# Opening: products of ones ahead of the first row, a row moved; a norm's root on VectorE and two holds dropped

## The chip, the cores and the metric

The kernel runs on one core of a Trainium2 chip. The engines are TensorE (PE; its weight loads are listed as PEld), VectorE (DVE), ScalarE (ACT), GpSimd (POOL) and SyncE (SP, used here for its DMA queue). The metric is device time of one execution in microseconds; the time before is a median of three runs.

## The reference

Two layers of a diffusion transformer with model width 1024 on 256 latent tokens (LAT) and 256 context tokens (CTX), all in fp32. Cut to what matters:

```python
mod_lat = split(silu(c) @ ada_w[i] + ada_b[i], 9)        # shift, scale, gate for three sublayers
mod_ctx = split(silu(c_ctx) @ ada_w[i] + ada_b[i], 9)
def half_ffn(h, shift, scale, gate, w_in, w_out, g, b):
    xm = h * (1 + scale) + shift
    a, u = split(xm @ w_in, 2)
    y = (silu(a) * u) @ w_out
    return layer_norm(ALPHA * h + 0.5 * gate * y, g, b)
# layer 0: half_ffn, grouped-query attention (+ post norm), half_ffn
# layer 1: half_ffn, mLSTM (+ post norm), half_ffn; h_lat is returned
layer_norm(x) = (x - mean) * rsqrt(var + 1e-5) * g + b
```

The FFN's hidden width is 2816. The four FFNs are called first to fourth here; the norm behind the second one ends layer 0, and the norm behind the third one stands ahead of the mLSTM.

## The kernel before, in words

**Layout and products.** The hidden state is kept transposed in SBUF, h[128, 8, 512]: eight tiles of 128 features, with columns 0 to 255 for LAT and 256 to 511 for CTX. Every matrix product is made as three fp32r products: high half of the weights by high half of the input, high by low, and low by high (`mm3`, L230, L233, L234). A weight tile is split by `split`: ACT writes the high half as a cast (L213), DVE subtracts it from the original to get the low half (L218), in one piece or in four slices of 256 columns. Raw weight tiles stand in a ring of four (`RAW`); SP issues their DMAs in order (L198), each waiting until the last slice of an earlier split has read the tile that it overwrites. The split pairs stand in a ring of seven.

**The opening (`start`).** The rows of silu(c) for LAT (v = 0) and CTX (v = 1) are needed on all 128 partitions, for dot products on DVE. PE spreads them (`replicate(v, i)`: four fp32 products of 128 columns for each half i of row v, into the PSUM tile rep[v][i]), and DVE copies them to SBUF (`replicated`, L1525). The shift (ch 0) and scale (ch 1) vectors of the first sublayer are then made tile by tile: some by PE (`by_pe`, eight fp32 products of two columns for each vector tile), the others by DVE dots (`by_dve`, L1542). With these, ACT and DVE modulate the input tile (`modulated`, L1555; low half at L1560), and `products(d)` makes 21 products of 512 columns for tile d with the first weights. Each fp32 product stands as two rows in the trace. The program order of PE, DVE and ACT is pinned by hand in this function.

**The norm behind an FFN (`norm`).** It is a generator; the last output units of the FFN and the first input units of the next one advance it by one step at places that tables of letters give. Its steps for each half (LAT, then CTX): the mean by PE; eight tiles of subtraction (DVE, L447) and squares (ACT, L454), summed by DVE or POOL (L466); the variance by PE; the root of its inverse for 256 tokens, as a 128 x 2 tile; a product of the identity with it (L492); PE spreads it over the partitions; eight tiles of scaled and modulated input with high and low halves (L517 to L524). The residual of the FFN's last units is added at L626 and summed at L402. The root is made in one of two ways: `root_log` on ACT with Ln and Exp (L271, L272) and one Newton step of three DVE operations (L273 to L275), for which ACT has to load another table (L262) and later the one for Silu again (L570); or `rsqrt_half` on DVE, an integer guess and three Newton steps of three operations. Which one is used is set by `log`: "load" loads the table ahead, "kept" uses what is loaded, and no entry takes DVE. The norm behind the second FFN uses "load" for LAT and "kept" for CTX.

**The hold (`tie`).** With `tie`, the last square of the LAT half becomes a fence: each later split's cast on ACT is ordered behind that square (`behind`, an edge of order only). The norms behind the second and the third FFN have it. Work that is not pinned is ordered by a tile scheduler.

## Time and profile before

| what | value |
|---|---|
| timed runs | 1642.85, 1645.7, 1650.05 us; median 1645.7 |
| profiled execution: time | 1653.1 us |
| profiled execution: span of the core | 1651.0 us |
| mean granted TensorE clock | 0.994 |
| PE busy | 1622.1 us (98%) |
| DVE busy | 1407.1 us (85%) |
| ACT busy | 751.8 us (46%) |
| POOL busy | 160.0 us (10%) |

The profile is of one execution of its own, not of a timed run; its time is the span and 2.1 us around it. A product of PE is listed with its full duration, though products overlap, so a pace is read from the number of rows in a stretch rather than from the mean duration. The granted clock is a share of full speed. In a row of a wait, the arrow points to what the engine waited for; in a row of the timeline, the bracket holds the idle time ahead of the row and what ended it.

### The profile page before, as it was taken

How to read it: one execution, taken by the hardware profiler on the slowest of the kernel's cores; microseconds unless marked ns; L12 is line 12 of the kernel's file. 1: busy time of each engine (PE TensorE's matmuls, PEld its weight loads, DVE VectorE, ACT ScalarE, POOL GpSimd, SP SyncE). 2: the span in 40 equal slices, each digit the busy share in tenths (PEclk: the TensorE clock that was granted, in tenths of full speed). 3: DMA queues.
4: the chain of work that ended last, by engine and by line, in shares of the span. 5: the costliest groups of instructions: out<-in, count | busy, mean ns of one | idle time of the engine just before them, and what ended most of it. 6: DMA issues, size and time to landing. Idle time of an engine off the chain costs nothing. (4 is left out here: it accounts for less than half of the span.)

```text
span 1651.0 us, 27330 instructions
## 1 busy us (share of the span) xinstructions
PE 1622.1 (98%) x10496; PEld 1475.7 (89%) x10496; DVE 1407.1 (85%) x2857; ACT 751.8 (46%) x1369; POOL 160.0 (10%) x237
## 2 busy tenths in 40 slices
PE   9999999999999999999999899999999999999998
PEld 8888888889988998899999898998999978999986
DVE  6899999979788998888796899898797967997686
ACT  4532123315676364254354453453453646556542
POOL 0011111102321200000000200000001002120000
PEclk9999999999999999999999899999999999999999
DMA  7777777732202444435333544335332342437552
GB/s 283 269 247 252 229 243 237 247 128 87 65 1 79 177 167 149 145 103 179 115 114 105 192 153 141 115 111 183 99 119 78 109 141 77 130 114 255 180 180 75
DMA packets 72210, 250.65 MB, mean 152 GB/s; under 512 B 7952, under 2 KB 11024, under 8 KB 72080
## 3 DMA queue, kind: packets, MB, share of 16 engines
q1 hardware_dynamic: 53360, 182.93, 33.0%
q0 software_dynamic: 17856, 65.02, 12.1%
q8 instruction: 82, 1.34, 0.3%
q10 hardware_dynamic: 864, 0.96, 0.2%
q14 instruction: 48, 0.39, 0.1%
HBM read 247.83 MB, written 1.05 MB: 151 GB/s over the span
## 5 line engine op out<-in xcount | busy, mean ns | idle before, releaser
L233 PE MATMUL t<-t,t 128*128 128x256 f32 (+2 forms) x2072 | 678.5, 329 | 1.2 <-DVE t L524 0.8
L234 PE MATMUL t<-t,t 128*128 128x256 f32 (+2 forms) x2072 | 674.6, 327 | 4.7 <-DVE t L218 4.6
L230 PE MATMUL t<-t,t 128*128 128x256 f32 (+2 forms) x2072 | 676.9, 329 | 1.8 <-ACT t L213 1.7
L213 ACT CAST t<-t 128x1024 fp32r<-128x1024 f32 (+2 forms) x390 | 329.2, 866 | 309.0 <-PE t L234 134.1
L218 DVE TENSOR_TENSOR t<-t,t 128x256 fp32r<-128x256 f32 (+2 forms) x726 | 415.8, 614 | 44.8 <-ACT t L213 43.0
L234 PEld LDWEIGHTS t<-t,t 128*128 128x128 f32 x2072 | 391.4, 189 | 39.9 <-DVE t L218 5.5
L233 PEld LDWEIGHTS t<-t,t 128*128 128x128 f32 x2072 | 392.6, 190 | 37.3 <-DVE t L524 1.7
L230 PEld LDWEIGHTS t<-t,t 128*128 128x128 f32 x2072 | 390.6, 190 | 38.1 <-ACT t L213 3.2
L827 PEld LDWEIGHTS t<-t,t 128*128 128x128 f32 x2436 | 288.4, 189 | 2.6 <-ACT t L835 0.6
L827 PE MATMUL t<-t,t 128*128 128x256 f32 x2436 | 289.4, 281 | 0.6 <-DVE t L848 0.4
L338 DVE SCALAR_TENSOR_TENSOR t<-t,t 128x1024 bf16<-128x1024 f32 x224 | 266.0, 1220 | 1.3 <-DMA t<-in_ada_w 1.1
L762 ACT CAST t<-t 128x512 fp32r<-128x512 f32 (+1 forms) x116 | 108.7, 941 | 148.4 <-DVE t L764 93.6
L330 POOL DMA_DIRECT2D t<-in_ada_w x124 | 66.5, 536 | 796.0 <-DVE t L338 734.5
L763 DVE TENSOR_TENSOR t<-t,t 128x512 fp32r<-128x512 f32 (+1 forms) x116 | 125.3, 1087 | 6.8 <-ACT t L762 6.1
L626 DVE SCALAR_TENSOR_TENSOR t<-t,t,t 128x256 f32<-128x256 f32 x128 | 56.7, 478 | 52.6 <-PE t L234 52.3
L1042 PE MATMUL t<-t,t 128*128 128x256 f32 (+1 forms) x256 | 78.2, 306 | 1.1 <-DVE t L218 1.1
L1041 PE MATMUL t<-t,t 128*128 128x256 f32 (+1 forms) x256 | 78.8, 309 | 0.0
L1043 PE MATMUL t<-t,t 128*128 128x256 f32 (+1 forms) x256 | 78.3, 308 | 0.0
L570 ACT ACTIVATE t<-t 128x256 f32<-128x256 f32 (+1 forms) x64 | 30.1, 479 | 104.0 <-PE t L234 101.0
L1496 PE MATMUL t<-t,t 128*128 128x512 f32 (+2 forms) x280 | 61.3, 381 | 3.2 <-ACT t L316 3.2
L1496 PEld LDWEIGHTS t<-t,t 128*128 128x128 f32 x280 | 53.7, 236 | 10.4 <-ACT t L316 3.2
L976 PE MATMUL t<-t,t 128*128 128x512 f32 x264 | 60.0, 389 | 0.0
(198 smaller groups left out, 1481.9 us busy)
## 6 DMA issues: line engine op xcount, KB each, us to landing
t<-in_ffn_in SPq DMA_DIRECT2D x168, 512.0 KB, 4.4
t<-in_ada_w POOLq DMA_DIRECT2D x124, 512.0 KB, 4.3
t<-in_ffn_out SPq DMA_DIRECT2D x68, 512.0 KB, 4.4
t<-in_ffn_last SPq DMA_DIRECT2D x22, 512.0 KB, 3.4
t<-in_ada_w SPq DMA_DIRECT2D x15, 512.0 KB, 8.3
t<-in_att_in SPq DMA_DIRECT2D x12, 512.0 KB, 3.9
t<-in_att_out SPq DMA_DIRECT2D x8, 512.0 KB, 3.4
t<-in_ml_qk SPq DMA_DIRECT2D x8, 512.0 KB, 3.7
```

Source lines behind the costliest of these rows:

```text
L213: self.behind(self.nc.scalar.copy(h, x))
L218: self.behind(self.nc.vector.tensor_tensor(out=ls, in0=xs, in1=hs.bitcast(F32), op=ALU.subtract))
L230: ins = mm(out, wh, xh, start=first, stop=False)
L233: mm(out, wh, xl, start=False, stop=False)
L234: mm(out, wl, xh, start=False, stop=last)
L338: ins = nc.vector.scalar_tensor_tensor(self.tmp().bitcast(BF16), r, 1.0, self.cb[:, v, :], ALU.mult, ALU.mult, accum_out=to)
L762: high = lambda p, r: pin(S.copy(p[0], r))
L763: low = lambda p, r: pin(V.tensor_tensor(out=p[1], in0=r, in1=p[0].bitcast(F32), op=ALU.subtract))
L827: pin(nc.tensor.matmul(o, p, q, start=first and k == i == 0, stop=k == half - 1 and i == 2, skip_group_check=True))
L1041: mm(o, self.xh[:, k, c], wh, start=k == 0, stop=False)
L1043: mm(o, self.xl[:, k, c], wh, start=False, stop=k == ND - 1)
L1496: mm = lambda *k, **kw: pin(nc.tensor.matmul(*k, **kw))
```

## The change

There are three parts. **(A)** In the opening, eight fp32 products of the constant ones by ones, 128 x 128, are put ahead of the first `replicate`; they write rep[1][1], which the second row of c overwrites later. Both halves of c's second row are replicated behind the scale vector's products (ch 1) and ahead of the shift vector's (ch 0), where one half stood behind each; DVE's copy of the last half moves ahead of the first weights' split. **(B)** The norm behind the second FFN makes its root with `rsqrt_half` on DVE for both halves, so no table is loaded for it, and its hold is dropped. **(C)** The norm behind the third FFN keeps its root on ACT and drops its hold. The parameter `tie` goes. The line numbers behind the edits move by one or two (L1496 becomes L1494, L1525 becomes L1523, L466 becomes L464, L492 becomes L490, L517 becomes L515, L626 becomes L624).

```diff
--- before.py
+++ after.py
@@ -418,7 +418,7 @@
             else:
                 self.advance(len(self.running) - 1 if c.isupper() else 0)
 
-    def norm(self, g, coef, keep=True, nxt=True, alone=False, log=False, tie=False):
+    def norm(self, g, coef, keep=True, nxt=True, alone=False, log=False):
 
 
         nc, V, S = self.nc, self.nc.vector, self.nc.scalar
@@ -451,9 +451,7 @@
                 S.activation(xh, z, AF.Copy, scale=c)
                 V.scalar_tensor_tensor(self.xl[:, d, TL:T], z, c, xh.bitcast(F32), ALU.mult, ALU.subtract)
             q = self.tmp(w)
-            square = S.activation(q, z, AF.Square)
-            if tie and d == ND - 1:
-                self.fence = {square.ins.engine: square}
+            S.activation(q, z, AF.Square)
             if d in (SQA if alone else SQPE):
                 sums[d] = q, q
                 continue
@@ -1530,7 +1528,8 @@
             for k in range(ND):
                 mm(o[ch], raws[d][ch][:, k * P : (k + 1) * P], b.ct[:, k, :], start=k == 0, stop=k == ND - 1)
             if ch in behind:
-                replicate(*behind[ch])
+                for i in range(2):
+                    replicate(behind[ch], i)
         for ch in o:
             pin(S.activation((e0, c0)[ch][:, :, d], o[ch], AF.Identity, bias=bias(ch, d)))
 
@@ -1564,18 +1563,20 @@
             for n, o in enumerate(acc):
                 mm(o, ws[d][w][:, n * P : (n + 1) * P], b.x(d, BOTH)[x], start=not d and not i, stop=d == ND - 1 and i == 2)
 
+    for i in range(ND):
+        mm(rep[1][1][:, :P], b.ones, b.ones, start=True, stop=True)
     for i in range(2):
         replicate(0, i)
         replicated(0, i)
     load_dots(0)
     load(0)
-    by_pe(0, {1: (1, 0), 0: (1, 1)})
-    replicated(1, 0)
+    by_pe(0, {1: 1})
+    for i in range(2):
+        replicated(1, i)
     low(ws[0][2], ws[0][0], ws[0][1])
     load_dots(1)
     rows = by_dve(1)
     next(rows)
-    replicated(1, 1)
     xs = {0: modulated(0)}
     for d in range(ND):
         n = d + 1
@@ -1662,9 +1663,9 @@
         tick.done = done
         return tick
 
-    def norm(key, coef, keep=(True, True), nxt=True, alone=False, log={LAT: "load", CTX: "kept"}, tie=False):
+    def norm(key, coef, keep=(True, True), nxt=True, alone=False, log={LAT: "load", CTX: "kept"}):
         get = once(key, coef)
-        b.begin = lambda g: b.norm(g, get, keep[0 if g == LAT else 1], nxt, alone, log.get(g), tie and g == LAT)
+        b.begin = lambda g: b.norm(g, get, keep[0 if g == LAT else 1], nxt, alone, log.get(g))
 
     both = (LAT, CTX)
     feeds = [feed(q, dots, 0 if i else ROOM[0][1]) for i, (q, dots) in enumerate(zip(queue, DOTS))]
@@ -1676,10 +1677,10 @@
     b.attention(lambda: b.shift_(0, 5))
     cpool = b.silu_c()
     b.pending = [lambda: b.silu_load(lambda ins: b.after(ins, b.silu) if ins.ins.engine == b.silu.ins.engine else ins)]
-    norm("n2", lambda: b.ln_mod(0, 2, (1, 0)), tie=True)
+    norm("n2", lambda: b.ln_mod(0, 2, (1, 0)), log={})
     b.ffn(0, 1, once("g1", lambda: b.half_gate(0, 8)), both, feeds[1])
     feeds[1].done()
-    norm("n3", lambda: b.ln_mod(1, 0, (1, 3)), (True, False), log={LAT: "load"}, tie=True)
+    norm("n3", lambda: b.ln_mod(1, 0, (1, 3)), (True, False), log={LAT: "load"})
     b.ffn(1, 0, once("g2", lambda: b.half_gate(1, 2)), both, feeds[2])
     feeds[2].done()
     cpool.close()
```

PE in the opening, before: t_86 to t_89 are the four halves of c's two rows, t_97 the shift and scale vectors, t_90 the first product of the input.

```order
L1496 MATMUL t_86<-t_70,t_72 128x128 x4
L1496 MATMUL t_87<-t_70,t_72 128x128 x4
L1496 MATMUL t_97<-t_72,t_111 128x2 x8
L1496 MATMUL t_88<-t_70,t_72 128x128 x4
L1496 MATMUL t_97<-t_72,t_111 128x2 x8
L1496 MATMUL t_89<-t_70,t_72 128x128 x4
L1496 MATMUL t_97<-t_72,t_147 128x2 x8
L1496 MATMUL t_90<-t_68,t_117 128x512
```

The same place after:

```order
L1494 MATMUL t_89<-t_61 128x128 x8
L1494 MATMUL t_86<-t_70,t_72 128x128 x4
L1494 MATMUL t_87<-t_70,t_72 128x128 x4
L1494 MATMUL t_97<-t_72,t_119 128x2 x8
L1494 MATMUL t_88<-t_70,t_72 128x128 x4
L1494 MATMUL t_89<-t_70,t_72 128x128 x4
L1494 MATMUL t_97<-t_72,t_119 128x2 x8
L1494 MATMUL t_97<-t_72,t_156 128x2 x8
L1494 MATMUL t_90<-t_68,t_125 128x512
```

The ones stand first; t_88 and t_89, the second row, are now both ahead of the second run of eight two-column products, so two such runs (and the tile behind, t_156) stand in a line ahead of the products.

ACT at the LAT half of the norm behind the second FFN, before: L454 are the squares, L213 the casts of the next FFN's weights, L271 and L272 the root.

```order
L213 CAST t_9158<-t_9156 128x1024
L454 ACTIVATE t_9180<-t_67 128x256
L454 ACTIVATE t_9183<-t_67 128x256
L454 ACTIVATE t_9188<-t_67 128x256
L454 ACTIVATE t_9191<-t_67 128x256
L454 ACTIVATE t_9196<-t_67 128x256
L454 ACTIVATE t_9200<-t_67 128x256
L454 ACTIVATE t_9204<-t_67 128x256
L454 ACTIVATE t_9234<-t_67 128x256
L213 CAST t_9493<-t_9491 128x1024
L213 CAST t_9525<-t_9523 128x1024
L271 ACTIVATE t_9263<-t_9256 128x2
```

The same place after:

```order
L213 CAST t_9166<-t_9164 128x1024
L213 CAST t_9505<-t_9503 128x1024
L454 ACTIVATE t_9187<-t_67 128x256
L454 ACTIVATE t_9190<-t_67 128x256
L454 ACTIVATE t_9195<-t_67 128x256
L454 ACTIVATE t_9198<-t_67 128x256
L213 CAST t_9537<-t_9535 128x1024
L454 ACTIVATE t_9203<-t_67 128x256
L454 ACTIVATE t_9207<-t_67 128x256
L454 ACTIVATE t_9211<-t_67 128x256
L454 ACTIVATE t_9241<-t_67 128x256
L213 CAST t_9599<-t_9597 128x1024
```

The first of the next FFN's casts (t_9505) stands ahead of the squares and the second (t_9537) between the fourth and the fifth; the two rows of the root are gone, and the table load (L262), which stood three rows ahead of the first piece, too.

DVE at the root of the same half, before: L486 gives the variance, L273 to L275 the Newton step, L218 are slices of the weights' splits, L492 the product with the identity.

```order
L486 SCALAR_TENSOR_TENSOR t_9256<-t_9249,t_9259 128x2
L218 TENSOR_TENSOR t_9493<-t_9491,t_9493 128x256 x2
L626 SCALAR_TENSOR_TENSOR t_67<-t_9280,t_6712,t_67 128x256
L218 TENSOR_TENSOR t_9493<-t_9491,t_9493 128x256
L402 TENSOR_TENSOR t_8993<-t_8993,t_67 128x256
L273 TENSOR_TENSOR t_9264<-t_9263 128x2
L218 TENSOR_TENSOR t_9525<-t_9523,t_9525 128x256
L274 TENSOR_TENSOR t_9264<-t_9264,t_9256 128x2
L218 TENSOR_TENSOR t_9525<-t_9523,t_9525 128x256
L275 SCALAR_TENSOR_TENSOR t_9263<-t_9264,t_9263 128x2
L218 TENSOR_TENSOR t_9525<-t_9523,t_9525 128x256
L492 TENSOR_TENSOR t_9270<-t_70,t_9263 128x256
```

The same place after, from the second Newton step on:

```order
L218 TENSOR_TENSOR t_9599<-t_9597,t_9599 128x256
L252 TENSOR_TENSOR t_9271<-t_9271,t_9263 128x2
L218 TENSOR_TENSOR t_9599<-t_9597,t_9599 128x256
L253 SCALAR_TENSOR_TENSOR t_9270<-t_9271,t_9270 128x2
L624 SCALAR_TENSOR_TENSOR t_67<-t_9316,t_6720,t_67 128x256
L251 TENSOR_TENSOR t_9271<-t_9270 128x2
L218 TENSOR_TENSOR t_9631<-t_9629,t_9631 128x256
L252 TENSOR_TENSOR t_9271<-t_9271,t_9263 128x2
L402 TENSOR_TENSOR t_9001<-t_9001,t_67 128x256
L253 SCALAR_TENSOR_TENSOR t_9270<-t_9271,t_9270 128x2
L218 TENSOR_TENSOR t_9631<-t_9629,t_9631 128x256
L490 TENSOR_TENSOR t_9282<-t_70,t_9270 128x256
```

Ten small steps (L249, and L251 to L253 three times) take the place of three, and the slices of a third and a fourth split (t_9599, t_9631) now stand among them; those of the first (t_9505) and second (t_9537) stand ahead.

## The prediction

> **What bounds the kernel now.** I read the page first, then the waits of the opening, then the windows of the stretches that the change touches. The page's engine list and clock row:
>
> ```profile
> span 1651.0 us, 27330 instructions
> PE 1622.1 (98%) x10496; PEld 1475.7 (89%) x10496; DVE 1407.1 (85%) x2857; ACT 751.8 (46%) x1369; POOL 160.0 (10%) x237
> PEclk9999999999999999999999899999999999999999
> ```
>
> PE is the bound: it leaves 29 us of 1651.0 idle, so time is won only where PE waits or runs at a slower pace. The clock row dips once, in the slice from 908 to 949 us. The waits of the first 40 us, by engine and releaser (total, times, longest), the timeline of the start, and PE's and DVE's busy time in its parts (stretch, length, PE, PEld, DVE, ACT, POOL, granted clock, DMA share, GB/s):
>
> ```profile
> DVE t L1525 <- PE t L1496: 7.4, 3, 4.4
> PE t L1496 <- ACT t L316: 3.2, 1, 3.2
> 0.79 0.17 DVE L283 MEMSET t<- 128x1 f32 x5 [0.79 <-PEq L1776]
> 2.95 0.22 ACT L316 ACTIVATE t<-t 128x16 f32<-128x16 f32 x1
> 12.76 1.08 DVE L1560 TENSOR_TENSOR t<-t,t 128x896 fp32r<-128x896 f32 x1
> 17.28 0.69 DVE L1525 COPY t<-t 128x512 f32<-128x512 f32 x1 [2.29 <-PE t L1496]
> 18.00 1.23 DVE L1542 SCALAR_TENSOR_TENSOR t<-t,t 128x1024 bf16<-128x1024 f32 x1
> 3.20:6.80 3.60, 3.58 (x17) 3.59 (x18) 0.76 (x2) 0.00 (x0) 0.00 (x0) 1.00 1.01 376
> 3.20:20.30 17.10, 17.09 (x80) 17.09 (x81) 7.24 (x14) 4.87 (x10) 0.00 (x0) 1.00 1.02 400
> 20.30:24.90 4.60, 4.60 (x12) 3.63 (x13) 4.56 (x9) 3.78 (x8) 0.00 (x0) 1.00 0.80 281
> 24.90:56.60 31.70, 31.70 (x157) 26.76 (x156) 31.38 (x61) 19.08 (x39) 0.00 (x0) 1.00 0.80 292
> 27.00:36.00 9.00, 9.00 (x42) 7.44 (x41) 8.93 (x17) 5.77 (x12) 0.00 (x0) 1.00 0.31 100
> ```
>
> PE idles only until 3.2 us, for the Silu of c on ACT. After that it is never idle, but it is slow: the 512-column products take 4.60/12 = 0.38 us from 20.3 to 24.9 and 9.00/42 = 0.214 us later (one of the twelve is a short row). The windows say 1.00 for both, so here I trust the pace rather than the clock column: PE runs the first 25 us at half pace. The 80 rows from 3.2 to 20.3 (each fp32 product is two) take 17.10/80 = 0.214 us each, and at full pace about 0.107. DVE, from its row at 18.00 on, is busy 31.38 of 31.70 us: from there the dots on DVE are as tight as PE.
>
> Now the norm behind the second FFN, in windows and waits:
>
> ```profile
> 925.00:930.00 5.00, 4.39 (x38) 4.18 (x36) 2.76 (x9) 1.80 (x4) 1.26 (x2) 1.00 0.98 319
> 930.00:935.00 5.00, 1.99 (x8) 1.95 (x9) 3.85 (x9) 2.32 (x6) 2.49 (x4) 0.79 0.81 280
> 935.00:940.00 5.00, 5.00 (x25) 5.00 (x25) 2.29 (x9) 1.88 (x5) 0.00 (x0) 0.50 0.83 303
> 940.00:945.00 5.00, 5.00 (x33) 5.00 (x33) 3.65 (x12) 2.27 (x6) 0.00 (x0) 0.69 0.68 215
> PE t L234 <- DVE t L218: 3.6, 1, 3.6
> PE t L425 <- DVE t L402: 0.9, 1, 0.9
> SPq L198 <- DVE t L218: 37.2, 3, 19.2
> ```
>
> PE stands still for 3.6 us, and behind that the granted clock is 0.79, 0.50 and 0.69 over 15 us: 5 x (0.21 + 0.50 + 0.31) = 5.1 us lost. Here PE waited for DVE's second half of a weight split, which waited for ACT, which waited for a transfer, which SP issued late since the raw tiles came free late (37.2 us of SP waits in three pieces, from 900 to 925).
>
> **The opening.** Added: eight fp32 products of ones, 16 rows. The first row of c took 3.58 us for as many rows, so I take 3.6 us. The ones are ready at 0.79 + 0.17 = 0.96, so they run from about 1.05 to 4.6; c is ready at 2.95 + 0.22 = 3.17. So c's first row starts 1.4 us later than at 3.21. That is the price. In return, dense rows stand from 1.05 to 8.2 without a break, 7.2 us. What such a stretch does to the pace is bounded by two rows: 3.58 us of dense fp32 rows (3.2 to 6.8) did not bring full pace, since the next 64 rows stayed at 0.21; 4.60 us of 512-column products did. No row shows fp32 rows alone raising the pace. Lower bound: they never do, and the opening loses 1.4 us. Upper bound: full pace 4.6 us after 1.05, at 5.7. I take 5.7 to 7.9, since 7.2 us of dense work is far nearer to the 4.60 that did than to nothing. Then the 80 old rows take: from 4.6 to 5.7 five at 0.214, 75 at 0.107 = 8.0, products at 13.7; with full pace at 7.9: 15 slow, 65 at 0.107 = 7.0, products at 14.9. Against 20.3 that is -6.6 or -5.4, and the 2.0 us that the slow products lose (4.60 - 12 x 0.214) come on top, if the pace holds through the 32 two-column rows in a line (3.4 us, hardly any columns), which I doubt.
>
> PE alone would thus win 7 to 8 us, but DVE's dots bind next. Their tight run starts with the second row of c at 18.00. In the new order c's second row is complete after 48 old rows instead of 64: 5.7 + 43 x 0.107 = 10.3 (or 7.9 + 33 x 0.107 = 11.4). DVE copies (0.69), then splits the first weights (1.08 at 12.76), then runs the first dot, which stood at 13.76 behind the split without a wait, so that its weight row had landed by then; if it lands no sooner, both dots stand at 13.76 and 15.0 (-3.0), and if the row is there when the split ends, at 12.2 and 13.4 (-4.6). I take -4.6, since no wait of DVE for that transfer is in the list. Beyond it DVE and ACT have a little lead to give up at the end of the run:
>
> ```profile
> 57.31 0.92 DVE L1560 TENSOR_TENSOR t<-t,t 128x256 fp32r<-128x256 f32 x2 [0.67 <-ACT t L1555]
> 64.36 0.39 PE L230 MATMUL t<-t,t 128*128 128x512 f32 x1
> ```
>
> ACT had the eighth modulated tile ready at 57.31. PE's 21 products with it end at 64.36, where the next line's begin, and so start near 64.36 - 21 x 0.214 = 59.9: a lead of 2.6 us, and with all of it used PE could win 7.2. I take **-5.7**, a little under half of the lead, from -7.5 (all of PE's own win) to -3.5 (the pace falls once in the two-column rows: 3.4 us at half pace cost 1.7, and only a quarter of the lead is used).
>
> [...]
>
> **The norm behind the second FFN.** Its root moves from ACT (Ln, Exp, three DVE steps) to ten DVE steps, and the weight casts are no longer held behind the eighth square. Rows of the LAT half, and of the CTX half:
>
> ```profile
> 900.25 1.41 ACT L454 ACTIVATE t<-t 128x256 f32<-128x256 f32 x4 [14.19 <-DVE t L447]
> 904.26 1.98 ACT L213 CAST t<-t 128x1024 fp32r<-128x1024 f32 x2
> 907.10 0.20 ACT L271 ACTIVATE t<-t 128x2 f32<-128x2 f32 x1 [0.87 <-DVE t L486]
> 909.27 0.16 DVE L274 TENSOR_TENSOR t<-t,t 128x2 f32<-128x2 f32 x1
> 910.08 0.42 DVE L492 TENSOR_TENSOR t<-t,t 128x256 f32<-128x256 f32 x1
> 908.68 14.48 SPq L198 DMA_DIRECT2D t<-in_ffn_in  x2
> 919.71 1.27 DVE L524 SCALAR_TENSOR_TENSOR t<-t,t,t 128x256 fp32r<-128x256 f32 x3
> 922.35 0.41 DVE L218 TENSOR_TENSOR t<-t,t 128x256 fp32r<-128x256 f32 x1
> 923.15 0.70 PE L425 MATMUL t<-t,t 128*128 128x256 f32 x2 [0.94 <-DVE t L402]
> 929.15 1.04 ACT L213 CAST t<-t 128x1024 fp32r<-128x1024 f32 x1 [3.20 <-DMA t<-in_ffn_in]
> 930.10 1.33 ACT L454 ACTIVATE t<-t 128x256 f32<-128x256 f32 x4
> 931.15 0.51 DVE L466 TENSOR_TENSOR t<-t,t 128x256 f32<-128x256 f32 x1 [3.39 <-ACT t L454]
> 938.67 1.28 ACT L570 ACT_TABLE_LOAD   x1
> 945.76 0.87 DVE L522 SCALAR_TENSOR_TENSOR t<-t,t,t 128x256 f32<-128x256 f32 x2 [2.11 <-PE t L425]
> ```
>
> Gain: with the hold gone the first cast (two from 904.26 before) runs ahead of the squares, where ACT was idle for 14.19 us, and the second between squares four and five. DVE has room for their splits ahead of the root, so the raw tiles come free near 890 and 908, by my chain of the new order, instead of near 908.7 and 922.7, where the last slice of the second split (922.35) and SP's two issues stand. SP issues the transfers that much earlier, and the cast at 929.15 finds its data; squares five to eight of the CTX half (930.10), queued behind it on ACT, and DVE's sum behind them (931.15) move with it. The 3.6 us stall goes, and with it the reason for the slow clock, 5.1 us: together -8.7, and -0.9 for L425's wait. Two table loads of 1.28 us on ACT go; the one at 938.67 stands ahead of the gated products' Silu, behind which PE shows no wait, so I count nothing.
>
> Price: ten small steps at about 0.16, with a split slice at its pitch of 0.33 between most of them, where the old root took 907.10 to 910.08 on both engines. The order puts eight slices and one residual step that waits for PE among them, and I reach 912.1 for the product with the identity, against 910.08: +2.0 us. The modulation chain of the LAT half, on DVE without a pause up to 920.98, moves by about 1.5 of it. PE's cover there is the FFN's last units, which end near 922.2 (923.15 less its wait of 0.94); past that point a delay is bare: by my chain 1.1 us at the first products, 1.0 at L425, and 0.6 for the CTX half's root. -9.6 + 2.7 = -6.9, and I take **-6.4**, since a transfer on POOL's queue can still hold up a cast a little. Bounds: -8, if the delays hide; 0, if they add up in one place and the clock falls again.
>
> **The norm behind the third FFN** keeps its table; only the hold goes, so the mLSTM's first casts come earlier:
>
> ```profile
> 1291.30:1294.70 3.40, 2.90 (x21) 2.56 (x22) 3.40 (x13) 1.60 (x3) 0.05 (x1) 1.00 0.25 104
> 1294.70:1298.10 3.40, 3.40 (x19) 3.40 (x18) 3.40 (x18) 1.46 (x3) 0.00 (x0) 0.50 0.73 186
> ```
>
> 0.5 us of idle and 1.7 of half clock stand there; it is hung on DVE (3.40 of 3.40), which gets the same work in another order. I take **-1**, from -2.4 to +0.5.
>
> **Sum.** -5.7 - 6.4 - 1 = -13.1 on the profiled execution, 1653.1 (span 1651.0), so 1640. But the three timed runs, 1642.85 to 1650.05 with median 1645.7, all lie below it. The half-clock stretches sum to 5.1 + 1.7 = 6.8, nearly the 7.4 between; where they fall depends on where an idle stretch meets the clock's own grid, so I count half of them as absent from a median run: -13.1 + 3.4 = -9.7, **1636.0 us**.
>
> **Rivals.** (1) The fp32 ones don't raise the pace. For it: 3.58 us did not. Opening +1.4, the two norms -4: 1643. (2) The pace rises and falls again in the two-column rows, and DVE eats the rest: opening -2.5, norms -4: 1639. (3) The other side: DVE's longer root lets the clock fall twice. The FFN's last units end near 922.2 and the first modulated pieces come 2 us later; the same holds behind the CTX root near 939. The idle of 3.6 us at 929 was enough for slow windows worth 5.1; if about 2 us at a stretch is enough, which decides here, the price is two slow stretches of 5.1 and two idles of 2.3 = 14.8 against 9.6 saved, +5.2, and with the opening at -3.5 and the third norm at +0.5 the end is 1648. Against it: PE has no idle wait in that stretch but the 0.9 us, and the delays as I chain them come to 1.1 at most at a time. (4) The casts come early, but SP's transfers are late anyway, since POOL's own weights fill the queues (DMA share 0.98 from 925 to 930): norms 0, opening -5.7: 1640.
>
> **Numbers.** Forecast 0.56, (1) 0.14, (2) 0.14, (3) 0.08, (4) 0.08. Range: down to 1629 (the whole 13.1 and the spread of 3.6 below a median), up to 1646.5 (rival 1 with the same spread). About 0.5%, 8.2 us, is what a timing of this kernel can tell from no change. Faster than 1637.5: 0.7 of the forecast, a third of (2), a fifth of (1) and (4) = 0.48, and I give 0.51 since both large terms could be whole; slower than 1653.9: 0.07, the tail of (3) and (1) by the spread of the runs; the rest, 0.42, within.
>
> **What would show it.** After: 512-column products of 0.214 us from the first on, the first near 14 us; c's second row copied near 11; no wait of DVE L218 above 2 us near 929, the granted clock 1.00 from 930 to 945, the cast's wait for in_ffn_in gone, the raw tiles' transfers issued near 890 and 908. It is wrong if the fp32 rows after the ones still take 0.21 us, or if PE waits more than 2 us near 921 with a clock below 1 behind it.

## The result, and the profile after

| | before | after |
|---|---|---|
| median, of 9 runs each on the same chip | 1650.05 us (1642.85 to 1655.72) | 1639.47 us (1639.01 to 1643.78) |
| ratio | | 0.9943, interval 0.9926 to 0.9960 |
| profiled execution, span | 1651.0 us | 1641.8 us |
| mean granted clock | 0.994 | 0.997 |

The gain is 0.57%, 9.4 us of 1650. The predicted time was 1636.0 in a range of 1629.0 to 1646.5. The three runs that were shown of before lie low in its spread, as its two lowest and its middle one: with six more its median rose from 1645.7 to 1650.05. The page of the kernel after, its span, engines and clock row:

```profile
span 1641.8 us, 27378 instructions
PE 1616.7 (98%) x10512; PEld 1469.7 (90%) x10512; DVE 1410.3 (86%) x2871; ACT 748.7 (46%) x1363; POOL 161.4 (10%) x237
PEclk9999999999999999999999999999999999999999
```

The dip in the clock row is gone. The opening after, in windows (stretch, length, PE, PEld, DVE, ACT, POOL, granted clock, DMA share, GB/s) and in the timeline (start, duration, engine, line):

```profile
8.20:10.00 1.80, 1.80 (x18) 1.80 (x18) 0.17 (x1) 0.46 (x1) 0.00 (x0) 1.00 1.04 404
12.00:14.00 2.00, 1.49 (x14) 1.41 (x13) 2.00 (x2) 1.03 (x4) 0.00 (x0) 0.96 1.02 413
16.00:18.00 2.00, 2.00 (x7) 1.71 (x8) 1.23 (x3) 1.97 (x5) 0.00 (x0) 0.50 1.05 423
22.00:24.00 2.00, 2.00 (x11) 1.65 (x10) 1.96 (x6) 0.17 (x1) 0.00 (x0) 1.00 1.02 413
0.91 3.79 PE L1494 MATMUL t<-t 128*128 128x128 f32 x16 [0.91 <-DVE t L283]
4.48 8.41 PE L1494 MATMUL t<-t,t 128*128 128x128 f32 x64
11.25 0.69 DVE L1523 COPY t<-t 128x512 f32<-128x512 f32 x1 [0.20 <-PE t L1494]
14.00 1.22 DVE L1541 SCALAR_TENSOR_TENSOR t<-t,t 128x1024 bf16<-128x1024 f32 x1
60.31 0.39 PE L230 MATMUL t<-t,t 128*128 128x512 f32 x1
```

The ones run as 16 rows from 0.91, and c's rows start at 4.48. From 8.2 to 10.0 PE has 18 rows in 1.80 us and is at full pace: from start to start the 128-column rows are 0.112 us apart here, and 0.213 before the rise. (A window also counts the rows that began ahead of it, so where rows are long the pace is better read from start to start.) Then it falls again: the first 512-column product comes at 16.47, behind the two-column rows, and from there to 20.2 these products are 0.427 us apart, at a granted clock of 0.50; from 22 on they are 0.227 us apart. The opening ends at 60.31 instead of 64.36, 4.05 us earlier. The norm behind the second FFN, after: windows, PE's waits there, SP's weight transfers, and rows of the timeline:

```profile
920.00:925.00 5.00, 4.89 (x40) 4.64 (x40) 5.00 (x15) 0.90 (x4) 1.59 (x3) 1.00 0.92 350
925.00:930.00 5.00, 4.63 (x40) 4.42 (x39) 5.00 (x11) 2.11 (x7) 3.16 (x5) 1.00 0.98 363
930.00:935.00 5.00, 5.00 (x46) 5.00 (x45) 5.00 (x19) 2.03 (x5) 0.16 (x1) 1.00 0.95 331
935.00:940.00 5.00, 4.15 (x33) 3.90 (x32) 4.62 (x16) 3.58 (x10) 0.00 (x0) 1.00 0.26 105
PE t L230 <- ACT t L568: 0.9, 1, 0.9
PE t L425 <- DVE t L464: 0.4, 1, 0.4
881.59 46.91 SPq L198 DMA_DIRECT2D t<-in_ffn_in  x7
899.98 1.05 ACT L213 CAST t<-t 128x1024 fp32r<-128x1024 f32 x1
910.10 0.43 DVE L490 TENSOR_TENSOR t<-t,t 128x256 f32<-128x256 f32 x1
925.95 1.41 ACT L454 ACTIVATE t<-t 128x256 f32<-128x256 f32 x4 [0.25 <-DVE t L447]
```

Seven of the next FFN's transfers are issued between 881 and 929 (before: five, from 883.40, in 44.42 us). The second cast stands at 899.98, between the squares. The squares of the CTX half run without a cast among them, the 3.6 us wait is gone, and the granted clock is 1.00 throughout.

Where the 9.2 us between the two profiled spans arose follows from pairing PE's rows of the two traces in order and taking the difference of their starts at several places:

| place (time in before) | after minus before, us |
|---|---|
| 70, behind the opening | -4.06 |
| 390, ahead of attention | -3.97 |
| 700, in the second FFN | -1.81 |
| 910 / 921, norm behind the second FFN | -1.80 / -1.11 |
| 1000, in the third FFN | -7.98 |
| 1350, in the mLSTM | -10.31 |
| the end | -9.14 |

So the opening gave 4.1, the norm behind the second FFN 6.2, the one behind the third about 2, and 2.2 us between 390 and 700 and 1.2 us after 1350 went the other way, where the edits changed nothing. The last section comes back to both.

### The profile page after: what moved, and what is told of

Same layout as the page of the kernel before. It is cut to its first block, busy times and chain, and to the rows that moved or that the text cites. A ratio compares the mean times of both kernels' runs of the same rounds, so it can differ in the third digit from the quotient of the medians.

```text
span 1641.8 us, 27378 instructions
## 1 busy us (share of the span) xinstructions
PE 1616.7 (98%) x10512; PEld 1469.7 (90%) x10512; DVE 1410.3 (86%) x2871; ACT 748.7 (46%) x1363; POOL 161.4 (10%) x237
## 3 DMA queue, kind: packets, MB, share of 16 engines
HBM read 247.83 MB, written 1.05 MB: 152 GB/s over the span
## 5 line engine op out<-in xcount | busy, mean ns | idle before, releaser
L230 PE MATMUL t<-t,t 128*128 128x256 f32 (+2 forms) x2072 | 675.3, 329 | 2.8 <-ACT t L213 1.7
L213 ACT CAST t<-t 128x1024 fp32r<-128x1024 f32 (+3 forms) x390 | 329.0, 866 | 315.9 <-PE t L234 143.3
L218 DVE TENSOR_TENSOR t<-t,t 128x256 fp32r<-128x256 f32 (+2 forms) x726 | 418.1, 619 | 47.0 <-ACT t L213 45.5
L230 PEld LDWEIGHTS t<-t,t 128*128 128x128 f32 x2072 | 387.5, 188 | 39.6 <-ACT t L213 3.2
L624 DVE SCALAR_TENSOR_TENSOR t<-t,t,t 128x256 f32<-128x256 f32 x128 | 56.9, 482 | 50.1 <-PE t L234 49.9
L974 PEld LDWEIGHTS t<-t,t 128*128 128x128 f32 x264 | 49.5, 188 | 10.2
L454 ACT ACTIVATE t<-t 128x256 f32<-128x256 f32 x72 | 25.9, 412 | 70.4 <-DVE t L447 70.4
```

Of the source, the lines that this page charges most:

```text
L213: self.behind(self.nc.scalar.copy(h, x))
L218: self.behind(self.nc.vector.tensor_tensor(out=ls, in0=xs, in1=hs.bitcast(F32), op=ALU.subtract))
L230: ins = mm(out, wh, xh, start=first, stop=False)
L974: pin(nc.tensor.matmul(ys[tt][i], gs[g], ws[k][w][:, i * 512 : (i + 1) * 512], start=k == 0 and g == w == 0, stop=k == NF - 1 and g == 1,))
```

## The experiments

Each kernel was timed in turn with the kernel before, on the same chip for the runs of one group. The groups are runs 1 to 4, 5 to 8 and 9 to 12; the medians of before in them were 1647.94 (35 runs), 1646.57 (29) and 1648.57 (22).

### The opening alone

```diff
+    for i in range(ND):
+        mm(rep[1][1][:, :P], b.ones, b.ones, start=True, stop=True)
     for i in range(2):
         replicate(0, i)
...
-    by_pe(0, {1: (1, 0), 0: (1, 1)})
+    by_pe(0, {1: 1})
```

> The opening's edits alone (ones, both halves of the second row moved), both norms as before. Theory 1 (the ones bring full pace early, it falls once in the two-column rows, DVE's dots take the rest): the products end near 60.3 instead of 64.4, the whole kernel -4 us, ratio 0.9975; the stall of 3.6 us and the half clock behind the second FFN stay. Rival (the opening's gain is given back later, since DVE or the DMA sets the first FFN): products end at 60.3, but the shift against before is gone by 380 us, ratio 1.000.

Measured: 1646.41 us, ratio 0.9976 (0.9959 to 0.9992), 12 runs. In its profile the first FFN starts 4.52 us earlier than in before, and the shift is still -4.44 at 390 and -3.67 at 897. So the opening's gain arrives at the end, and the rival falls. What I did not expect is its norm, which is that of before. PE's wait there and two windows:

```profile
PE t L234 <- DVE t L218: 1.3, 1, 1.3
925.00:930.00 5.00, 3.74 (x31) 3.39 (x30) 4.38 (x11) 0.89 (x2) 1.91 (x4) 1.00 0.98 360
930.00:935.00 5.00, 5.00 (x44) 4.95 (x44) 5.00 (x18) 3.51 (x8) 0.00 (x0) 1.00 1.05 365
```

With unchanged code the wait was 1.3 us instead of 3.6, and no half clock followed. The stall that I priced at 8.7 us is not the same in every execution: from 880 to 1000 us this kernel, with the norm of before, gains 7.8 us on the profile of before, more than the 6.2 of the changed kernel.

### The two norms alone

```diff
-    norm("n2", lambda: b.ln_mod(0, 2, (1, 0)), tie=True)
+    norm("n2", lambda: b.ln_mod(0, 2, (1, 0)), log={})
...
-    norm("n3", lambda: b.ln_mod(1, 0, (1, 3)), (True, False), log={LAT: "load"}, tie=True)
+    norm("n3", lambda: b.ln_mod(1, 0, (1, 3)), (True, False), log={LAT: "load"})
```

> The two norms' edits alone (root on DVE behind the second FFN, both holds dropped), opening as before. Theory 1 (the casts that run earlier take the stall and with it the half clock away): no granted clock below 1 between 25 us and the end, -6 us behind the second FFN, -2 behind the third, ratio 0.995 to 0.996. Rival (the half clock falls where the grid puts it, and a median run of before hardly has it): -2 us, ratio 0.9985.

Measured: 1644.0 us, ratio 0.9976 (0.9962 to 0.9990), 12 runs: between the two, 4 us. In its profile the clock is 1.00 from 23.2 to 1637.7 us, 4 us from the end, as theory 1 wants, and the shift grows by 6.2 us behind the second FFN. The median gains less than the profiled pair, probably since many executions of before have no slow stretch to lose: of the five profiles with the holds, two have none behind the second FFN. And its opening, which is that of before, runs otherwise than in the profile of before:

```profile
6.20:9.60 3.40, 3.40 (x33) 3.40 (x32) 1.23 (x3) 0.37 (x1) 0.00 (x0) 1.00 0.98 351
9.60:13.00 3.40, 3.40 (x17) 3.40 (x17) 2.75 (x4) 1.28 (x4) 0.00 (x0) 0.50 1.04 418
20.00:23.20 3.20, 3.20 (x9) 2.52 (x8) 3.16 (x8) 1.19 (x3) 0.00 (x0) 0.50 1.04 422
```

Without any ones, PE takes 33 rows in 3.4 us from 6.2 on, full pace, and falls to 17 rows in the next 3.4. The 3.58 us of fp32 rows from 3.21 did raise the clock here, at 6.2; in the profile of before they did not, and it rose at 24.9. The column of the clock shows 1.00 ahead of its first record too (in before at 24.94), so that 1.00 in the first microseconds says nothing. The same opening reached full pace at 24.9, 6.2, 7.2 and 6.8 us in four profiles. The places at which the clock changes are worked out from the traces further down.

### The root alone

```diff
-    norm("n2", lambda: b.ln_mod(0, 2, (1, 0)), tie=True)
+    norm("n2", lambda: b.ln_mod(0, 2, (1, 0)), log={}, tie=True)
```

> Only the root behind the second FFN moves to DVE; both holds stay, opening as before. Theory 1 (the hold, not the root, made the casts late): the cast in front of squares five to eight of the CTX half still waits about 3 us for its transfer, PE stands still 3 to 6 us there, the half clock stays, and the longer root adds 1 to 2: ratio 1.000 to 1.002. Rival (the root frees ACT and the table loads cost the time): the stall goes, -5 us, ratio 0.997.

Measured: 1648.86 us, ratio 0.9994 (0.9979 to 1.0010), 12 runs: no change. The stall stays, in pieces of 1.3, 0.7 and 1.1 us of waits, and the clock falls behind it:

```profile
PE t L425 <- DVE t L466: 1.3, 1, 1.3
925.00:930.00 5.00, 2.66 (x19) 2.06 (x17) 3.57 (x7) 1.36 (x2) 2.39 (x4) 1.00 0.92 321
930.00:935.00 5.00, 4.95 (x32) 4.96 (x33) 4.41 (x21) 0.00 (x0) 0.00 (x0) 0.72 0.78 264
```

PE is busy 2.66 of 5 us, and a clock of 0.72 follows. The root by itself, with two table loads less, wins nothing that can be measured.

### The holds alone

```diff
-    norm("n2", lambda: b.ln_mod(0, 2, (1, 0)), tie=True)
+    norm("n2", lambda: b.ln_mod(0, 2, (1, 0)))
...
-    norm("n3", lambda: b.ln_mod(1, 0, (1, 3)), (True, False), log={LAT: "load"}, tie=True)
+    norm("n3", lambda: b.ln_mod(1, 0, (1, 3)), (True, False), log={LAT: "load"})
```

> Only the two holds are dropped; the root behind the second FFN stays on ACT with its two table loads, opening as before. Theory 1: the casts move ahead of the squares, the transfers are issued earlier, the stall goes and no half clock follows; -7 to -9 us, ratio 0.995, as good as with the root moved or 1 us better since the root is 2 us shorter. Rival (the root is what wins): the stall and the half clock stay, ratio 1.000.

Measured: 1643.48 us, ratio 0.9972 (0.9958 to 0.9985), 12 runs: as much as both norm edits together, though less than the 7 to 9 us that I expected. The difference of the means to the kernel with both norm edits, in the same group, is -0.4 us, with an interval of -2.0 to +1.3 (the 12 and 12 runs drawn again with repetition; the differences below are made in the same way). So by time the dropped holds, which were not tried one by one, carry the gain of the norms. The mechanism is only in part the expected one: the clock does not fall, but the stall is not gone. A cast between the squares of the CTX half still waits for its transfer, and PE behind it:

```profile
923.60 1.05 ACT L213 CAST t<-t 128x1024 fp32r<-128x1024 f32 x1 [0.74 <-DMA t<-in_ffn_in]
PE t L425 <- DVE t L466: 1.5, 1, 1.5
```

### The ones alone

```diff
+    for i in range(ND):
+        mm(rep[1][1][:, :P], b.ones, b.ones, start=True, stop=True)
```

> The ones alone; the second row's halves stay behind the scale and the shift products, norms as before. Theory 1 (the ones bring full pace for every position of the clock's grid, and dense and sparse rows then alternate so that about a third of a window is dense): full pace from 5 to 7.5, a fall once between 10 and 14, products end 60.5 to 61.5, ratio 0.998 to 0.999. Rival (what wins is the second row's earlier copy, so that DVE's dots start earlier): ratio 1.000 to 1.001, since the ones cost 1.4 us.

Measured: 1642.51 us, ratio 0.9974 (0.9962 to 0.9987), 12 runs. That is the whole gain of the opening, more than I expected of it; the rival falls. In its windows the pace rises and falls as in the kernel after:

```profile
6.00:12.80 6.80, 6.80 (x63) 6.80 (x63) 4.14 (x5) 2.15 (x5) 0.00 (x0) 1.00 1.02 397
12.80:19.60 6.80, 6.80 (x23) 5.84 (x23) 6.69 (x16) 6.50 (x14) 0.00 (x0) 0.50 1.03 413
```

The first FFN starts 5.22 us earlier than in before. The norm of this profile, which has the hold, shows the old stall at its full size: a wait of 4.2 us and a clock of 0.76, 0.50 and 0.72 in three windows of 5 us.

### The move alone

```diff
-    by_pe(0, {1: (1, 0), 0: (1, 1)})
-    replicated(1, 0)
+    by_pe(0, {1: 1})
+    for i in range(2):
+        replicated(1, i)
```

> The second row's halves moved ahead of the shift products, no ones; norms as before. Theory 1: the pace rises only where the grid lets a window lie inside 3.2 to 6.8, as in some runs of before; DVE's dots start 1.7 to 3.4 us earlier, of which 1 to 2 us arrive: ratio 0.999. Rival (the earlier copy is what wins): ratio 0.9975, as much as both edits together.

Measured: 1646.16 us, ratio 0.9995 (0.9977 to 1.0013), 12 runs: no change. In its profile full pace came only at 25.4 us, and the first FFN started 0.57 us later than in before:

```profile
18.00:25.00 7.00, 7.00 (x25) 6.13 (x26) 4.85 (x11) 6.81 (x15) 0.00 (x0) 1.00 0.79 301
25.40:30.00 4.60, 4.60 (x22) 3.78 (x21) 4.56 (x9) 2.05 (x5) 0.00 (x0) 1.00 0.41 145
```

From start to start the 512-column products are 0.427 us apart up to 25.4, and 0.227 behind it. The earlier copy of the second row, from which I derived the 4.6 us of DVE's dots, is worth nothing that can be measured by itself: in this profile PE is busy for the whole 7.00 us of the first window, so the products wait for nothing there and are only slow.

### The changed kernel with the gap filled

```diff
+            for i in range(ND if n == 1 else 0):
+                mm(acc[0][:, :P], b.ones, b.ones, start=True, stop=True)
             by_pe(n)
```

> The changed kernel with eight more products of ones between the two runs of two-column products, so that no window of 3.4 us is more than half sparse. Theory 1: the granted clock stays at 1.00 from about 6 us on, the first products run at 0.214 us, and after 1.7 us of filling the opening still ends 1 to 1.5 us earlier than in the changed kernel: products end near 59, ratio 0.9935. Rival (DVE's dots bind by then, so that pace wins nothing and the filling is bare): products end at 60 to 61, ratio 0.9945 to 0.995.

Measured: 1639.48 us, ratio 0.9954 (0.9938 to 0.9970), 5 runs. The mechanism is as expected:

```profile
12.20:15.60 3.40, 3.40 (x33) 3.40 (x32) 3.17 (x7) 3.37 (x9) 0.00 (x0) 1.00 1.02 414
15.60:19.00 3.40, 3.40 (x17) 2.83 (x17) 2.82 (x4) 3.37 (x9) 0.00 (x0) 1.00 1.03 414
ACT t L1554 <- DVE t L1544: 13.9, 4, 3.7
```

From 5.4 us the clock does not fall any more in the opening (the first 512-column products are 0.227 us apart, where the kernel after has 0.427), and the first FFN starts 6.5 us earlier than in before, against 4.06 for the profile of after. ACT now waits 13.9 us in four pieces for DVE's dots (12.2 in the profile of after), so little seems to be left that a quicker PE could use. The time is that of the changed kernel, but stands in another group; the run with both in one group is below.

### The changed kernel with the root on ACT

```diff
-    norm("n2", lambda: b.ln_mod(0, 2, (1, 0)), log={})
+    norm("n2", lambda: b.ln_mod(0, 2, (1, 0)))
```

> The changed kernel with the root behind the second FFN back on ACT (table loads and all); opening and dropped holds as in the change. Theory 1 (the holds win, the root is worth nothing): ratio 0.9945, within 0.1% of the changed kernel. Rival (the root on DVE carries a part of the gain that shows only with the new opening): ratio 0.996 to 0.997.

Measured: 1643.05 us, ratio 0.9979 (0.9964 to 0.9995), 12 runs. That is nearer to the rival than to theory 1, and above both. The filled kernel of the same group is 3.6 us faster in the mean (1.3 to 6.0), but it differs by the filling too. Its waits behind the second FFN, the cast on ACT, and the window:

```profile
PE t L425 <- DVE t L464: 2.6, 1, 2.6
ACT t L213 <- DMA t<-in_ffn_in: 1.9, 1, 1.9
923.79 1.05 ACT L213 CAST t<-t 128x1024 fp32r<-128x1024 f32 x1 [1.86 <-DMA t<-in_ffn_in]
924.75 1.33 ACT L454 ACTIVATE t<-t 128x256 f32<-128x256 f32 x4
925.00:930.00 5.00, 2.40 (x13) 2.19 (x12) 4.20 (x10) 1.08 (x4) 2.48 (x4) 0.80 0.92 332
```

Here the scheduler has left a cast between the squares of the CTX half, as in the run with the holds alone. It waits 1.86 us for its transfer, the last four squares stand behind it, and PE waits 2.6 us in one piece, with a clock of 0.80. With the root on DVE no cast stands there: in the profile of after the squares run to 925.95 + 1.41 in two blocks of four.

### The changed kernel again

Nothing is edited.

> The changed kernel once more, to stand beside the three others of this call with the same runs of before. Theory 1 (the parts add up: 0.9976 for the opening by 0.9976 for the norms): ratio 0.995. Rival (the parts help each other): 0.994 or less.

Measured: 1639.84 us, ratio 0.9944 (0.9922 to 0.9965), 7 runs: the first result again. The parts alone multiply to 0.9976 x 0.9976 = 0.9952, inside the interval; that they help each other is not shown. In this profile full pace lasted from 4.0 to 14.2 us, fell for 3.4 us only, and the first FFN started 6.05 us earlier than in before.

### The filled kernel again

> The changed kernel with eight more products of ones between the two runs of two-column products, again, with more runs and beside the changed kernel. Theory 1 (no fall of the clock in the opening): 1.5 to 2 us faster than the changed kernel, ratio 0.994 where that has 0.995. Rival (DVE's dots take it back): the same ratio as the changed kernel.

Measured: 1638.98 us, ratio 0.9944 (0.9925 to 0.9964), 8 runs. Against the changed kernel of the same group the difference of the means is -0.05 us (-1.6 to +1.5). The filling keeps the clock up and wins nothing that can be measured; the profiles would let it win 1 us (58.1 against 59.1 at the end of the opening, in the means of the table below), which is inside that interval.

### The changed kernel without the move

```diff
-    by_pe(0, {1: 1})
+    by_pe(0, {1: (1, 0), 0: (1, 1)})
```

> The changed kernel with the second row's halves back behind the scale and the shift products; ones and norms as in the change. Theory 1 (the ones carry the opening, the move nothing): ratio 0.995, the same as the changed kernel within 0.1%. Rival (the move carries a part): 0.9965 to 0.997.

Measured: 1640.27 us, ratio 0.9952 (0.9931 to 0.9973), 8 runs; the difference to the changed kernel is +0.7 us (-0.7 to +2.0). The move carries nothing that can be measured. In this profile the clock stayed up through the whole opening without any filling, and the first FFN started 7.5 us earlier than in before, the most of all profiles (9.1 us at 30, of which DVE and ACT let 7.5 arrive at 64):

```profile
11.30:14.70 3.40, 3.40 (x27) 3.17 (x26) 3.33 (x7) 3.40 (x7) 0.00 (x0) 1.00 1.02 416
14.70:18.10 3.40, 3.40 (x17) 2.79 (x16) 3.40 (x6) 2.96 (x8) 0.00 (x0) 1.00 1.03 408
```

The same opening fell at 12.8 in the run with the ones alone.

### The filled kernel with the root on ACT

> The filled kernel with the root behind the second FFN back on ACT. Theory 2 (formed on the run with the root on ACT: there the scheduler leaves a cast between the squares of the CTX half, it waits 1.9 us for its transfer, PE stands 2.6 us in one piece and the clock falls in some runs): PE waits 1.5 to 3 us in one place near 925, and the ratio is 0.002 above that of the filled kernel, about 0.996. Rival (the root is worth nothing, the earlier difference was noise): the same ratio within 0.1%.

Measured: 1641.01 us, ratio 0.9953 (0.9933 to 0.9973), 12 runs; PE's waits behind the second FFN:

```profile
PE t L425 <- DVE t L464: 2.5, 1, 2.5
PE t L425 <- DVE t L402: 0.6, 1, 0.6
```

The wait in one piece is there again, as theory 2 has it, 2.5 us against 1.3 in the filled kernel. The clock did not fall behind it in this execution. The time is 1.5 us above the filled kernel's (-0.4 to +3.3), which does not exclude nothing and is a little less than half of theory 2's 0.002 (3.3 us). So the wait is shown, and what it is worth stays open: 1.5 us here, 3.6 in the group before, nothing with the old opening (-0.4).

## Why the prediction was right or wrong

**The clock, by profile.** The runs together tell more than any of them. First the opening: when PE reached full pace, when it fell and when it came back, and when the first product behind the opening (L230) starts, all from the granted clock and PE's rows of the profiles:

| kernel | full from | falls | back at | opening ends |
|---|---|---|---|---|
| before | 24.9 | | | 64.4 |
| move alone | 25.4 | | | 64.9 |
| norms alone | 6.2 | 9.6 | 23.2 | 61.9 |
| root alone | 7.2 | 10.6 | 20.8 | 60.8 |
| holds alone | 6.8 | 10.2 | 20.4 | 60.6 |
| change | 7.0 | 13.8 | 20.7 | 60.3 |
| change again | 4.0 | 14.2 | 17.6 | 58.3 |
| opening alone | 6.1 | 12.9 | 19.7 | 59.8 |
| change, root on ACT | 6.4 | 13.3 | 20.1 | 60.1 |
| ones alone | 6.0 | 12.8 | 19.6 | 59.1 |
| change without the move | 4.5 | | | 56.9 |
| filled; again; with root on ACT | 5.4; 6.1; 6.2 | | | 57.8; 58.2; 58.3 |

Without ones the opening ends at 62.5 in the mean of five profiles, with ones and no filling at 59.1 in the mean of six, with filling at 58.1 in three.

How the same opening runs otherwise each time can be read with the record of the clock. Its shortest stretch in the profile of before is 3.413 us long (half clock, from 1294.70 to 1298.12), and in every profile all its changes lie whole multiples of this apart (in before, 24.94, 932.89, 943.13 and 1294.70 us: 0, 266, 269 and 372 times; in after, 7.01, 13.84, 20.67 and 1638.58 us: 0, 2, 4 and 478 times). So this grid can be carried back to the start, which is an estimate, and the time that rows of 128 or more columns fill in each of its windows can be added up. Without ones, the first such rows stand from 3.21 to 6.79. In the three profiles that rose early they fill 2.95, 3.04 and 3.41 us of the window that ends with the rise; in before and in the move alone the best window up to 18 us holds 2.33 and 1.88 us, by the position of the grid alone. With the ones, these rows stand from 0.91 to about 7.5, and all nine profiles have a window filled for 3.07 us or more, which ends with the rise. In these openings no window with 2.69 us or less raised a slow clock. The falls go the same way: up to 25 us, full-pace windows with 1.30 us or less of such rows were followed by a fall, those with 1.62 or more were not. That also parts the run without the move (1.62 or more in each) from the ones alone (1.25 ahead of the fall at 12.8).

Then the norms: of the five profiles with the holds, the clock fell behind the second FFN in three (for 10.2, 10.2 and 3.4 us) and behind the third in four (3.4 us each); of the nine without, behind the second in one (3.4 us, root on ACT) and behind the third in two. (Falls elsewhere stand in two profiles: at 1454 us in the root alone, at 552 in the filled kernel again.) Against the profile of before, the stretch from 880 to 1000 us is shorter by 3.7 us in the mean of the five profiles with the holds (0.0 to 7.8, before itself counted as 0) and by 6.5 in the mean of the nine without (4.9 to 7.6); the stretch from 1270 to 1350 by 0.1 (-0.1 to 0.3) and by 1.6 (0.4 to 2.2). The differences, 2.7 and 1.5 us, come to the 4 us that the norms gave by time.

**The opening, -5.7 forecast.** Right in the mechanism: the ones bring full pace early, at 4.0 to 7.0 us in all nine profiles with them. The ones start at 0.91 and c's rows at 4.48 (1.05 and 4.6 were said), the fp32 rows raise the pace (7.0 us, within 5.7 to 7.9), the second row is copied by 11.25 + 0.69 (near 11). It was mis-sized in two terms, and the first 512-column product came at 16.47 where the sum had 13.7 to 14.9. The pace fell once in the two-column rows, which I doubted rightly but kept out of the value taken; and the term that I took, DVE's dots 4.6 us earlier, came to 4.0 (18.00 to 14.00) and is not owed to the moved row: the move alone, which should have brought a part of it, brought nothing, and without the move the same dot started at 13.13. A reading was off too, with little effect: the 0.38 and 0.214 us for a 512-column product came from counts of windows, and from start to start they are 0.427 and 0.227. In profiles the opening gained 4.05 (after) and 6.05 (again). By time it gained 0.24%, 4.0 us. The larger slip lies in the base: "3.58 us of dense fp32 rows did not bring full pace" was true of the profile of before and not of the kernel. In three of five profiles without ones they did, by where the grid fell, so the ones change how surely full pace comes early, and the mean gain is 62.5 - 59.1 = 3.4 us, not the gain against the worst case.

**The norm behind the second FFN, -6.4 forecast.** In the profiled pair it was -6.2, and its steps came as said: the product with the identity stands at 910.10, 1.8 us later than before's 910.08 less the shift of 1.81 there (2.0 was said); the transfers are issued at 889.0 and 905.9, or 890.8 and 907.7 with the shift (near 890 and 908 were said); the stall and the half clock are gone; the small waits of PE are 0.9 and 0.4 (1.1, 1.0 and 0.6 were said). Three steps failed.

First, I put the half clock into the sum as if it belonged to the kernel, and then took half of it out again for the median; by time both norms together gave 4 us (0.9976), where -6.4 - 1 + 3.4 = -4.0 was the sum: the discount was right in size. The clock's grid, which the sum gives as its reason, is in the records above; that it keeps half of the slow stretches out of a median run was an estimate of mine, and no run shows that share: of the five profiles with the holds, the clock fell behind the second FFN in three and behind the third in four.

Second, I took the stall of 3.6 us as fixed, and it is a draw as well. The cast between the CTX squares waits for one transfer, which SP issues between 922.4 and 922.8 us in the time of before (with the root on DVE about 2 us later). How long it took to land, in the profile of before and in that of the opening alone, whose norm is the same (KB, us to landing):

```profile
t<-in_ffn_in SPq DMA_DIRECT2D x1, 512.0 KB, 6.2
t<-in_ffn_in SPq DMA_DIRECT2D x1, 512.0 KB, 3.7
```

PE's longest wait behind the second FFN goes with it, with the holds and without:

| kernel | a cast between the CTX squares | its transfer, us to landing | PE's longest wait, us |
|---|---|---|---|
| before; ones alone | yes | 6.2; 6.7 | 3.6; 4.2 |
| opening alone; move alone | yes | 3.7; 3.5 | 1.3; 0.8 |
| root alone | yes, one square behind it | 6.6 | 1.3 |
| holds alone | yes | 3.8 | 1.5 |
| change, root on ACT; filled, root on ACT | yes | 4.9; 4.8 | 2.6; 2.5 |
| norms alone; change; again; without the move; filled, twice | no | 4.2 to 6.6 | 0.7 to 1.3 |

What makes that transfer land late in one execution and not in the next is not shown.

Third, the root was booked as a price of 2.7 us of waits, and the dropped hold as what lets the cast find its data. The table has it otherwise: with the hold dropped and the root on ACT the cast stays between the squares and still waits, and it is the root on DVE that then takes it out, through the order that the scheduler chooses. With the hold kept (the root alone), the cast still stands ahead of the last square. What that is worth by time stays open: with the root on ACT the kernel is not slower with the old opening (by -0.4 us, -2.0 to +1.3), and with the new one slower by 1.5 (-0.4 to +3.3) and by 3.6 (1.3 to 6.0, beside the filled kernel). That the holds alone win 0.28% is measured; how much of it lies behind the second FFN is not, as the three profiles with the holds dropped and the root on ACT gain 4.9 to 7.6 us there, and two of those with the holds gain 6.5 and 7.8. So the -6.2 of the profiled pair, so near to -6.4, is in part luck.

**The norm behind the third FFN, -1 forecast.** The profiled pair shows -2, within the bounds. Its share of the time was not measured alone; the mean of the profiles above makes it 1.5 us.

**The sum and the median.** -9.7 us was forecast for a median, and 9.4 is what the ratio gives. That they lie so near is in part luck. The -13.1 of the profiled pair became -9.2: the opening gave 1.6 less, the third norm 1 more, and 3.4 us were lost in stretches that no edit touches (-4.06 to -1.81, and -10.31 to -9.14). The absolute time came out 3.5 us above the forecast, as the base had been three runs with a median 4 us below the later one. It lies inside the range. And the parts alone gave 4.0 us each by time, 8 in all, where the sum, less its discount for the norms, had 5.7 and 4.0; the 9.4 of the whole is within the noise of both.

**The rivals.** (1), that the fp32 ones raise nothing, is excluded by every profile with ones. (2), that the pace falls again in the two-column rows, is what happened in five of six unfilled profiles; its second half, that DVE takes the rest, shows in part: where the clock stayed up without filling, 1.6 of 9.1 us were gone by the end of the opening. (3), that the clock falls twice, did not happen. (4), that SP's transfers are late anyway, is excluded as a cost of the change, where seven instead of five are issued by 929: one of them, issued at 922.59, took 6.1 us to land, but no cast stood between the squares to wait for it. The kernel with the root on ACT still had a wait of 1.9 us of that kind.

## What to carry to other kernels

A profile is one draw: where a slow stretch hangs on the clock or on the landing of one transfer, look for it in several profiles of the same code before it is booked as a cost, and book its mean. Here work that only keeps PE busy was worth its place (ratio 0.9974 for the ones alone) where PE would have stood idle anyway, ahead of the first operand's arrival at 3.17 us; more of it, in the middle of the opening, kept the clock up as well and won nothing that could be measured. It takes about 1.8 us of PE itself (an estimate: 16 rows at 0.112). An order-only hold on one engine's work can be dear through the queue behind it: here casts that waited for nothing kept raw tiles from coming free, and so a transfer queue from issuing (in before it waited 37.2 us for the splits), and without the two holds the ratio was 0.9972. And an edit on one engine can matter by the order that a scheduler then gives to another: look at the new order before booking only its cost.

## What was not expected of the hardware

Products of 256 columns follow each other at two paces at a full granted clock, 0.113 and 0.118 us from start to start, and a stretch of the same code can have the one in one execution and the other in the next. Windows in attention and in the second FFN's beginning, the first two of before, the other two of after:

```profile
410.00:430.00 20.00, 20.00 (x177) 19.91 (x176) 19.74 (x65) 14.85 (x43) 4.02 (x4) 1.00 0.24 72
600.00:615.00 15.00, 15.00 (x122) 14.51 (x121) 13.53 (x33) 9.20 (x18) 2.71 (x5) 1.00 0.69 246
```

```profile
410.00:430.00 20.00, 20.00 (x172) 20.00 (x171) 18.12 (x63) 14.12 (x48) 4.02 (x4) 1.00 0.40 129
600.00:615.00 15.00, 15.00 (x110) 14.20 (x109) 14.03 (x37) 8.87 (x17) 2.12 (x4) 1.00 0.84 297
```

By the shift, a window of the same times does not hold quite the same products, so the rows themselves were paired: the 119 rows from 600 to 615 of before take 14.76 us in before and 15.23 in after. The median from one start to the next is 0.113 us in these stretches of before and 0.118 in after, without a wait. With it went about 1.3 of the 2.2 us between 390 and 700; another 1.1 arose at one place, near 556, in the norm ahead of the second FFN, where PE waited 0.5 us for VectorE and 0.2 for GpSimd in after and not at all in before. In all thirteen other profiles the stretch from 390 to 700 took longer than in before, by 0.04 to 2.2 us, so before's profile was a lucky draw there. The 1.2 us behind 1350 arose from 1485 to 1515, with medians of 0.113 in before and 0.118 in after. The second profile of the changed kernel has 0.113 there, and from 548 to 556 before is the slower one (0.118 against 0.114): the pace moves in both directions between executions. What chooses it was not tried. So it is part of the spread of before, 1642.0 to 1655.83 over all 95 runs.
